# All SBUF buffers whose size is a multiple of 128 bytes begin at multiples of 128 bytes

## The chip, the cores and the metric

The kernel runs on one core of a Trainium2 chip. The metric is the device time of one execution in microseconds (us). The kernel before was timed three times: 1064.94, 1066.04 and 1066.87 us, median 1066.04 us. One more execution was recorded by the hardware profiler; all rows below come from that one.

## What is computed

A decoder trunk of two layers on 256 tokens with 1024 features, in float32. Each layer is an FFN, a token mixer and a second FFN, every one behind an RMSNorm whose scale, shift and gate come from a vector `c`:

```python
for l in range(DEPTH):                                    # 2
    mod = (c_act @ w_ada[l] + b_ada[l]).reshape(B, 3, 3, D_MODEL)
    h = ada_norm(x, norm_g[l, 0], mod[:, 0, 0], mod[:, 0, 1])
    x = x + 0.5 * mod[:, 0, 2][:, None, :] * swiglu(h, ffn_w13[l, 0], ffn_w2[l, 0])
    h = ada_norm(x, norm_g[l, 1], mod[:, 1, 0], mod[:, 1, 1])
    x = x + mod[:, 1, 2][:, None, :] * token_mixer(h, w_in[l], ...)   # NSA | FoX | MoBA heads
    h = ada_norm(x, norm_g[l, 2], mod[:, 2, 0], mod[:, 2, 1])
    x = x + 0.5 * mod[:, 2, 2][:, None, :] * swiglu(h, ffn_w13[l, 1], ffn_w2[l, 1])
return rms_norm(x, final_g)
```

`swiglu(h, w13, w2)` is `(silu(a) * b) @ w2` with `a, b = split(h @ w13)`, and the hidden width is 2816. The 256 MB that the core reads from memory are nearly all weights: every weight is used once.

## The kernel before

**Tokens and weights.** The 256 tokens are two tiles of 128, called token tile 0 and 1 (`t` in the code). Activations are the stationary operand of a matmul (loaded into TensorE by a weight load of its own), the model's weights are the moving operand (streamed through it). Each weight chunk of 128 partitions x 1024 floats (4096 bytes in each partition) is loaded into one of seven `raw` buffers by the sync engine's DMA queue. ScalarE writes its rounded high part to one of eight `whi` buffers, VectorE the remainder to one of eight `wlo` buffers (`parts`), both of type fp32r. The activations are split in the same way: `hThi0`, `hTlo0` hold the transposed normalised input of token tile 0 in eight blocks of 128 floats, `hThi1`, `hTlo1` that of token tile 1; `gThi`, `gTlo` (three buffers each) hold the transposed hidden activations of either token tile.

**A product** is three matmuls (`mm3`): high x high, high x low, low x high. In TensorE's rows a name such as `ps_pc<-wlo,hThi` gives the PSUM bank, then the moving operand (`wlo`), then the stationary one (`hThi`). Numbers at the end of a name are left out in the profile, so `hThi` stands for `hThi0` and for `hThi1`; which it is follows from the place in the program.

**Order.** FFN: eleven groups `j` of 256 hidden features. `G1(j, t, ks)` multiplies token tile `t` with `w13`: three matmuls of 512 columns for each of the blocks `k`, 24 in all for `k` = 0 to 7; `G2` multiplies the hidden activations with `w2`. In the middle of an FFN (`steady`) `G1` goes through `k` and takes the two token tiles in turn, three matmuls each, 48 in all. At an FFN's end and start (`end`, `start`), where one token tile is still being normalised, `G1` runs with one token tile alone: 24 matmuls with `hThi0`, `hTlo0` in `end` (`G1(j, 0, K8)`), then 18 with `hThi1`, `hTlo1` (`G1(j, 1, K8[2:])`). The mixer's projections (`proj`, `oproj`) also take one token tile at a time. The instructions are recorded as a list, and a planner in the kernel (`schedule`, with a table of offsets `MOVES`) sets each engine's order and which buffer of a kind is used; nothing in it looks at addresses.

**Where buffers lie.** `Program.tile` asks the pool for the buffers of a kind when the kind's name comes up for the first time. The pool puts each buffer behind the one before, at the next multiple of 32 bytes in the partition. Small buffers (a 864-byte table, many of 32, 24 or 4 bytes) stand between large ones, so large ones begin wherever the small ones leave off. In the built program the first buffer, `x0`, begins at byte 16512 = 129 x 128. Start of each kind, in bytes past a multiple of 128:

| kinds | before | after |
|---|---|---|
| `whi`, `wlo` (moving operands), `nq` | 96 | 0 |
| `hThi0`, `hTlo0` (token tile 0) | 32 | 0 |
| `hThi1`, `hTlo1` (token tile 1), `gThi`, `gTlo` | 96 | 0 |
| `onesr`, `ident`, `nk` | 64 | 0 |
| `raw`, `gate`, `ms`, `zbmo` | 32 | 0 |
| `xn`, `nf`, `sg`, `gg`, `tk`, `vals` | 96 | 0 |
| `x0`, `x1`, `ones`, `crow`, `u`, `pt` | 0 | 0 |

The blocks of `hThi` and its like begin 512 bytes apart, the two halves of a `whi` buffer 2048 bytes apart, so every block of 512 columns has its buffer's figure.

Of the kernel before, what the change touches and what calls it, by code (L numbers as in the profile page):

```python
# [7 lines left out]
F32 = mybir.dt.float32  # L8
F32R = mybir.dt.float32r
# [277 lines left out]
class Program:  # L287
# [9 lines left out]
            k.made = []  # L297

    def tile(self, pool, shape, dt, name, bufs=1, loose=False, psum=False):
        if name not in self.kinds:  # L300
            self.kinds[name] = Kind([pool.tile(shape, dt, name=f"{name}_{i}" if bufs > 1 else name)
                                     for i in range(bufs)], loose)
        kind = self.kinds[name]
        b = Buf(len(self.bufs), kind, psum)
        self.bufs.append(b)
        return View(b, kind.tiles[self.plan[1][b.i] if self.plan else 0])
# [298 lines left out]
GROUPS1 = [2, 2, 2, 1, 1]  # L605
NRAW, NHL, NMS, NPT = 7, 8, 4, 4
S0, S1 = 21, 33


@with_exitstack  # L610
# [1186 lines left out]
```

## Time and profile before

| | |
|---|---|
| three timed runs | 1064.94, 1066.04, 1066.87 us |
| the profiled execution's own time | 1065.23 us |
| its span, first to last instruction | 1063.5 us |
[...]
| read from memory | 255.96 MB, 242 GB/s over the span |
| TensorE matmuls | 5060, of them 3864 with 512 columns of fp32r |

TensorE's matmuls are pipelined: a row's duration (390 to 411 ns for 512 columns) is longer than the time from one start to the next. What a matmul costs is that step from start to start. It is read from the chain of waits, which follows the work that ended last back through the program: a piece such as "5.60 PE ps_pc x24" is 24 matmuls in a row, and 5.60 us / 24 = 233.3 ns is the step.

### The profile page before, as it was taken

What the parts mean: (1) busy time and instruction counts of PE and PEld (TensorE: products, weight loads), DVE (VectorE), ACT (ScalarE), POOL (GpSimd) and SP (SyncE); (2) the same over time, 40 slices, a digit from 0 to 9 for tenths busy, and PEclk for the clock granted to TensorE, in tenths of its full rate; (3) what the DMA queues carried; (4) which work ended last, traced back from release to release, by engine and by line L of the source; (5) the groups of instructions that cost most, each with busy time, mean ns of one, the idle gap of its engine ahead of it and who ended that gap; (6) DMA issues with size and microseconds to landing.
All of it is one profiled execution on the core that took longest, in us unless ns stands there. A gap on an engine that the chain in (4) does not pass through costs nothing.

```text
span 1063.5 us, 14643 instructions
## 1 busy us (share of the span) xinstructions
PE 1041.4 (98%) x5060; PEld 838.7 (79%) x5060; DVE 830.9 (78%) x1561; ACT 603.3 (57%) x1094; POOL 27.7 (3%) x63
## 2 busy tenths in 40 slices
PE   5999999999999999999999999999999999999997
PEld 3888888888777788788888888887877788888885
DVE  6999988779998887788587667758999778556554
ACT  5564354567887644535485444447677766444442
POOL 3000000000000100000000000000000010000000
PEclk9999999999999999999999999999999999999999
DMA  9999999567663698899548777854758247666611
GB/s 341 371 324 367 377 337 327 191 206 243 204 227 123 223 339 318 291 339 336 198 168 283 256 268 257 284 210 154 236 180 264 93 149 277 210 206 210 209 65 39
DMA packets 71468, 257.97 MB, mean 243 GB/s; under 512 B 8193, under 2 KB 8193, under 8 KB 71394
## 3 DMA queue, kind: packets, MB, share of 16 engines
q1 hardware_dynamic: 70850, 256.12, 68.8%
q0 software_dynamic: 544, 0.93, 0.4%
q8 instruction: 39, 0.64, 0.2%
q14 instruction: 35, 0.29, 0.1%
HBM read 255.96 MB, written 1.05 MB: 242 GB/s over the span
## 4 chain that ended last, share of the span: by engine, by line
PE 87%; DVE 7%; DMA 2%; ACT 2%; issue 1%; POOL 1%; SPq 0%; POOLq 0%; DVEq 0%; ACTq 0%
PE ps_pc L561 51%; PE ps_pa L561 15%; PE ps_pb L561 14%; PE ps_tr L561 7%; DVE wlo L561 3%; DMA raw<-in_w_dram 2%; DMA x<-in_x_dram 1%; ACT whi L561 1%; DVE raw L561 1%; DVE nf L561 0%; POOL ss L561 0%; DVE u L561 0%; ACT xn L561 0%; DVE hTlo L561 0%; SPq L561 0%
## 5 line engine op out<-in xcount | busy, mean ns | idle before, releaser
L561 DVE TENSOR_TENSOR wlo<-raw,whi 128x1024 fp32r<-128x1024 f32 (+1 forms) x342 | 410.8, 1216 | 129.0 <-ACT whi L561 127.4
L561 ACT ACTIVATE whi<-raw 128x1024 fp32r<-128x1024 f32 (+1 forms) x342 | 356.7, 1053 | 200.1 <-PE ps_pc L561 107.6
L561 PE MATMUL ps_pc<-whi,hThi 128*128 128x512 f32 (+1 forms) x872 | 347.6, 399 | 0.4 <-ACT gates L561 0.3
L561 PE MATMUL ps_pc<-whi,hTlo 128*128 128x512 f32 (+1 forms) x872 | 340.7, 391 | 0.0
L561 PE MATMUL ps_pc<-wlo,hThi 128*128 128x512 f32 (+1 forms) x872 | 340.5, 390 | 0.0
L561 PEld LDWEIGHTS ps_pc<-whi,hThi 128*128 128x128 f32 x872 | 163.9, 188 | 37.2 <-issue 1.8
L561 PEld LDWEIGHTS ps_pc<-whi,hTlo 128*128 128x128 f32 x872 | 163.7, 188 | 36.7 <-DVE hTlo L561 0.2
L561 PEld LDWEIGHTS ps_pc<-wlo,hThi 128*128 128x128 f32 x872 | 164.0, 188 | 33.3
L561 DVE CUSTOM_DVE_ANT_0 raw<-raw,crow 128x1024 f32<-128x1024 f32 x96 | 115.6, 1221 | 7.2 <-DMA raw<-in_wada_dram 7.2
L561 ACT ACTIVATE gThi<-ps_tr 128x256 fp32r<-128x256 f32 x88 | 32.7, 383 | 74.4 <-PE ps_tr L561 74.2
L561 ACT ACTIVATE sg<-ps_pc 128x256 f32<-128x256 f32 x82 | 31.5, 384 | 75.8 <-PE ps_pc L561 75.5
L561 PE MATMUL ps_pa<-whi,gThi 128*128 128x512 f32 x184 | 73.5, 399 | 0.0
L561 PE MATMUL ps_pb<-whi,gThi 128*128 128x512 f32 x176 | 72.4, 411 | 0.0
L561 PE MATMUL ps_pa<-whi,gTlo 128*128 128x512 f32 x184 | 72.0, 391 | 0.0
L561 PE MATMUL ps_pa<-wlo,gThi 128*128 128x512 f32 x184 | 71.8, 390 | 0.0
L561 PE MATMUL ps_pb<-whi,gTlo 128*128 128x512 f32 x176 | 69.1, 393 | 0.0
L561 PE MATMUL ps_pb<-wlo,gThi 128*128 128x512 f32 x176 | 68.7, 390 | 0.0
L561 DVE SCALAR_TENSOR_TENSOR gate<-raw,cact,gate 128x1024 f32<-128x1024 f32 x48 | 61.4, 1279 | 6.6 <-DMA raw<-in_wada_dram 6.6
L561 ACT ACTIVATE ms<-ms,nm 128x128 f32<-128x128 f32 (+1 forms) x96 | 42.6, 446 | 16.5 <-DVE nm L561 16.5
L561 DVE TENSOR_TENSOR gg<-ps_pc,sg 128x256 f32<-128x256 f32 x82 | 33.5, 420 | 20.8 <-ACT sg L561 19.6
L561 DVE TENSOR_TENSOR gTlo<-ps_tr,gThi 128x256 fp32r<-128x256 f32 x88 | 36.0, 420 | 16.9 <-ACT gThi L561 16.9
L561 PEld LDWEIGHTS ps_pa<-whi,gTlo 128*128 128x128 f32 x184 | 34.5, 188 | 7.5
(257 smaller groups left out, 1085.8 us busy)
## 6 DMA issues: line engine op xcount, KB each, us to landing
raw<-in_w_dram SPq DMA_DIRECT2D x264, 512.0 KB, 4.9
raw<-in_wada_dram SPq DMA_DIRECT2D x144, 512.0 KB, 4.8
raw<-in_win_dram SPq DMA_DIRECT2D x40, 512.0 KB, 4.3
raw<-in_wc_dram SPq DMA_DIRECT2D x16, 512.0 KB, 3.5
raw<-in_wout_dram SPq DMA_DIRECT2D x16, 512.0 KB, 5.1
raw<-in_win_dram SPq DMA_DIRECT2D x4, 426.0 KB, 3.1
x<-in_x_dram SPq DMA_DIRECT2D x2, 512.0 KB, 6.6
out_dram<-xn SPq DMA_DIRECT2D x4, 256.0 KB, 2.1
```

What stands on the lines that cost most here:

```text
L561: return getattr(self.eng, op)(*[plain(a) for a in args], **{k: plain(v) for k, v in kw.items()})
```

## The change

Before the first kind that stands in a table `HOMES` is made, all kinds of the table are made, in the table's order. The table holds all kinds whose size is a multiple of 128 bytes, and the first of them, `x0`, begins at a multiple of 128; so each begins at one. All other kinds follow behind them as before. In the built program the instructions of every engine, their order, their waits and the choice among the buffers of a kind are the same as before; only the addresses in the operands differ. The space taken is 228,352 bytes of each partition in both.

```diff
@@ -297,6 +297,10 @@
     def tile(self, pool, shape, dt, name, bufs=1, loose=False, psum=False):
+        if name not in self.kinds and name in HOMES:
+
+            for n, (s, d, b) in HOMES.items():
+                self.kinds[n] = Kind([pool.tile(s, d, name=f"{n}_{i}" if b > 1 else n) for i in range(b)], False)
         if name not in self.kinds:
             self.kinds[name] = Kind([pool.tile(shape, dt, name=f"{name}_{i}" if bufs > 1 else name)
                                      for i in range(bufs)], loose)
@@ -605,6 +609,23 @@
+HOMES = {
+    "x0": ([128, 1024], F32, 1), "x1": ([128, 1024], F32, 1), "ones": ([128, 128], F32, 1),
+    "ident": ([128, 128], F32, 1), "onesr": ([128, 128], F32R, 1), "mask": ([128, 384], F32, 1),
+    "lower": ([128, 128], F32, 1), "cmask": ([128, 2, 16], F32, 1), "vals": ([128, 2, 12, 64], F32, 1),
+    "fqk": ([128, 2, 8, 66], F32, 1), "kcT": ([128, 2, 16], F32, 1), "kcs": ([128, 2, 2, 16], F32R, 1),
+    "hexp": ([128, 2, 4, 2, 16], F32, 1), "crow": ([128, 1024], F32, 1), "gate": ([128, 1024], F32, 2),
+    "cs": ([128, 2, 2, 16], F32, 1), "xn": ([128, 1024], F32, 1), "zbmo": ([128, 4, 256], F32, 1),
+    "hThi0": ([128, 8, 128], F32R, 1), "hTlo0": ([128, 8, 128], F32R, 1), "raw": ([128, 1024], F32, 7),
+    "nf": ([128, 256], F32, 2), "whi": ([128, 1024], F32R, 8), "wlo": ([128, 1024], F32R, 8),
+    "tk": ([128, 4, 512], F32, 1), "hThi1": ([128, 8, 128], F32R, 1), "hTlo1": ([128, 8, 128], F32R, 1),
+    "sg": ([128, 256], F32, 2), "gg": ([128, 256], F32, 2), "gThi": ([128, 2, 128], F32R, 3),
+    "gTlo": ([128, 2, 128], F32R, 3), "nq0": ([128, 4, 256], F32R, 1), "nq1": ([128, 4, 256], F32R, 1),
+    "u": ([128, 512], F32, 2), "nk0": ([128, 2, 256], F32R, 1), "nk1": ([128, 2, 256], F32R, 1),
+    "vbd": ([128, 8, 64], F32, 1), "wc2": ([128, 256], F32, 1), "ra": ([128, 8, 16], F32, 1),
+    "rb": ([128, 8, 16], F32, 1), "ms": ([128, 384], F32, 4), "pt": ([128, 384], F32, 4),
+}
```

## Rows read from the trace of the kernel before

**Rows 1.** The page: busy us (share), instructions; busy tenths in 40 slices.

```profile
PE 1041.4 (98%) x5060; PEld 838.7 (79%) x5060; DVE 830.9 (78%) x1561; ACT 603.3 (57%) x1094; POOL 27.7 (3%) x63
...
PE   5999999999999999999999999999999999999997
...
PEclk9999999999999999999999999999999999999999
DMA  9999999567663698899548777854758247666611
```

**Rows 2.** TensorE's waits, whole span: us in total, times, longest.

```profile
PE ps_pc L561 <- DVE tk L561: 6.4, 1, 6.4
PE ps_pc L561 <- DMA gate<-in_c_dram: 2.3, 1, 2.3
PE ps_pc L561 <- POOL bmask L561: 2.1, 1, 2.1
PE ps_tr L561 <- ACT xn L561: 2.0, 2, 1.2
...
PE ps_pa L561 <- DVE wlo L561: 0.2, 1, 0.2
```

**Rows 3.** The page: the chain that ended last, by engine.

```profile
PE 87%; DVE 7%; DMA 2%; ACT 2%; issue 1%; POOL 1%; SPq 0%; POOLq 0%; DVEq 0%; ACTq 0%
```

**Rows 4.** Chain in order of time (start us, us, what): FFN middles, tiles in turn.

```profile
116.87 11.15 PE ps_pc L561 x48
...
445.56 11.15 PE ps_pc L561 x48
...
947.00 11.15 PE ps_pc L561 x48
```

**Rows 5.** Same view: token tile 0 alone (`hThi0`, `hTlo0`).

```profile
186.21 5.60 PE ps_pc L561 x24
...
866.27 9.80 PE ps_pc L561 x42
```

**Rows 6.** Same view: token tile 1 alone (`hThi1`, `hTlo1`).

```profile
198.88 4.08 PE ps_pc L561 x18
...
557.97 5.48 PE ps_pc L561 x24
...
882.88 6.84 PE ps_pc L561 x30
```

**Rows 7.** Same view: `G2`, stationary operand `gThi`, `gTlo`.

```profile
531.95 4.08 PE ps_pb L561 x18
```

**Rows 8.** Same view: mixer 2, `proj` of 284 columns, then `cmp_h` of 256 columns.

```profile
756.09 1.96 PE ps_pc L561 x15
758.05 3.74 PE ps_pb L561 x32
```

**Rows 9.** Stretches: us, busy (x) of PE, PEld, DVE, ACT, POOL; clock, DMA share, GB/s.

```profile
30.00:60.00 30.00, 30.00 (x131) 24.27 (x130) 29.18 (x53) 14.67 (x21) 0.00 (x0) 1.00 1.00 368
...
100.00:200.00 100.00, 100.00 (x445) 80.84 (x444) 87.73 (x136) 43.62 (x58) 0.00 (x0) 1.00 0.93 338
...
900.00:1000.00 100.00, 100.00 (x447) 80.94 (x446) 57.94 (x65) 45.27 (x60) 0.00 (x0) 1.00 0.64 214
```

**Rows 10.** VectorE by shape: busy us, mean ns of one | idle before.

```profile
L561 DVE TENSOR_TENSOR wlo<-raw,whi 128x1024 fp32r<-128x1024 f32 x336 | 405.3, 1221 | 125.5 <-ACT whi L561 123.9
...
L561 DVE TENSOR_TENSOR x<-x,u 128x512 f32<-128x512 f32 x22 | 15.1, 689 | 0.4
...
L561 DVE TENSOR_TENSOR hTlo<-xn,hThi 128x512 fp32r<-128x512 f32 x4 | 2.7, 687 | 0.7 <-ACT hThi L561 0.6
```

**Rows 11.** ScalarE by shape, same columns.

```profile
L561 ACT ACTIVATE whi<-raw 128x1024 fp32r<-128x1024 f32 x336 | 351.9, 1056 | 198.0 <-PE ps_pc L561 105.5 <-DMA raw<-in_w_dram 43.4 <-PE ps_pb L561 37.6
...
L561 ACT ACTIVATE xn<-x 128x512 f32<-128x512 f32 x24 | 15.1, 628 | 20.1 <-DVE x L561 17.7 <-DMA x<-in_x_dram 2.4
...
L561 ACT ACTIVATE hThi<-xn 128x512 fp32r<-128x512 f32 x4 | 2.5, 624 | 0.0
```

**Rows 12.** Chain of 390 to 440 us, by line.

```profile
by line: DMA raw<-in_w_dram 33.7%; DVE wlo L561 27.0%; DVE raw L561 13.8%; ACT whi L561 6.4%; issue 5.7%; DVE gg L561 3.4%; DVE gTlo L561 3.0%; PE ps_pb L561 2.8%; PE ps_pa L561 2.7%; ACT gThi L561 0.8%; PE ps_tr L561 0.5%; ACTq L561 0.2%; 
```

**Rows 13.** The page: weight loads; DMA issues (KB each, us to landing).

```profile
L561 PEld LDWEIGHTS ps_pc<-whi,hThi 128*128 128x128 f32 x872 | 163.9, 188 | 37.2 <-issue 1.8
...
raw<-in_w_dram SPq DMA_DIRECT2D x264, 512.0 KB, 4.9
```

**Rows 14.** Chain in order of time: the first DMA piece.

```profile
3.77 9.70 DMA x<-in_x_dram
```

## The prediction

> **What bounds the kernel now.** I read the page first. [...] A busy TensorE may still be a waiting one, since its durations overlap; so next its waits. They are about 14 us in total, 10.8 of them in three single waits before the first weight matmul, and a wait for `wlo` shows up once, with 0.2 us [rows 2]. The chain that ended last agrees: 87% of it is TensorE [rows 3]. So the time is, to a first approximation, the number of matmuls times the step from one start to the next, and the change can matter through that step. Everything else has cover: VectorE and ScalarE wait for each other and for TensorE (the largest wait of `whi` is for TensorE, to give a buffer free) [rows 10, 11].
>
> So I read the steps, from chain pieces that hold nothing but 512-column matmuls. With the two token tiles in turn a step is 11.15 us / 48 = 232.3 ns, at 117, at 446 and at 947 us alike [rows 4]. With token tile 0 alone it is 5.60 / 24 = 233.3 ns, and 9.80 / 42 = 233.3 ns 680 us later [rows 5]. With token tile 1 alone it is 4.08 / 18 = 226.7, 5.48 / 24 = 228.3 and 6.84 / 30 = 228.0 ns, together 16.40 / 72 = 227.8 ns [rows 6]. `G2` has 4.08 / 18 = 226.7 ns [rows 7]. These matmuls have the same shape, types and moving operand (`whi`, `wlo`), and the same order of high and low parts. A weight load takes 188 ns [rows 13], less than any step, and loads the same 128 x 128 floats in all of them. What differs is the stationary operand's address: 32 bytes past a multiple of 128 for token tile 0, 96 for token tile 1 and for `G2`, while the moving operand always lies at 96. The step does not follow the other engines: the 232.3 ns are the same in the stretch of 100 to 200 us, where DMA is busy for 0.93 and VectorE for 0.88, and in that of 900 to 1000 us with 0.64 and 0.58 [rows 4, 9]. So I take it that the place of the stationary operand against the moving one sets 5.5 ns of the step: 227.8 ns where both lie at the same distance past a multiple of 128, 233.3 ns where they don't.
>
> **The change, part by part.** No instruction is added, removed or moved, so no queue is passed and no wait added. There are only new addresses, engine by engine.
>
> TensorE: after the change moving and stationary operands all lie at 0. If the distance between them decides, all steps become 227.8 ns. The 2736 matmuls with `hThi` or `hTlo` are 1632 with the token tiles in turn (8 groups x 48 in each of three FFNs, 10 x 48 in the first one) and 1104 with one alone, 552 for each token tile.
> - Token tile 0 alone: 552 x (233.3 - 227.8) ns = 3.0 us.
> - In turn: 1632 x (232.3 - 227.8) ns = 7.3 us. The row to aim at is that of one token tile alone, since both have the operand sequence in common. At the low end only the 816 steps of token tile 0 gain, 816 x 4.5 ns = 3.7 us.
> - Token tile 1 alone and `G2` (552 + 1104 steps) stay. At the high end they, and all the others, come down to the best piece, 226.7 ns: 552 x 6.6 + 1632 x 5.6 + 552 x 1.1 ns = 13.4 us in all.
> - The 24 matmuls with `onesr` and the small shapes: 24 x 5.5 ns = 0.1 us; left out.
>
> That is 10.3 us of TensorE's time. Not all of it is on the path: of 390 to 440 us the chain runs through `raw` landing (33.7%) and `wlo` (27.0%), and hardly through TensorE [rows 12]; there a quicker matmul ends sooner and what it gains is given back as a wait for `wlo`. The same holds at the changes from one stage to the next, where the chain runs through a norm. I take the chain's share of TensorE, 87% [rows 3], as what arrives: 9.0 us.
>
> VectorE and ScalarE: their large operands move too. Rows of the same shape with operands at other places bound this: `x<-x,u`, all at 0, takes 689 ns, `hTlo<-xn,hThi`, at 96 and 32, takes 687 ns [rows 10]; `xn<-x`, read at 0, 628 ns, `hThi<-xn`, read at 96, 624 ns [rows 11]. So nothing, by -2 to +4 ns in some 340 splits of 1221 and 1056 ns, hidden behind TensorE. Without that cover 4 ns x 336 would be 1.3 us.
>
> DMA: `raw` moves from 32 to 0, `x` stays at 0. Before 17 us TensorE waits for transfers, and the chain's first DMA piece (9.70 us) is `x`, which doesn't move [rows 14]. The trace shows no large load that differs in its place alone; a chunk lands 4.9 us after its issue [rows 13]. DMA is 2% of the chain [rows 3], 21 us; a twentieth either way is 1 us. I take 0, since the engines were already at 368 GB/s from 30 to 60 us without TensorE waiting [rows 9].
>
> The sum, against the profiled execution: 1065.23 - 9.0 = 1056.2 us. The median of the three runs lies 0.8 us above that execution, so the forecast is **1057 us**, with its own range from 3.0 + 3.7 us x 0.87 = 5.8 us of gain (1060) to 13.4 us (1052.6).
>
> [...] What the rows show is two steps for two places, 227.8 and 233.3 ns [rows 5, 6]. [...]
>
> **The rivals.**
>
> *Not the place past 128, but something that comes with the token tile* (15%). `hThi0` and `hTlo0` lie right below `raw`, `hThi1` and `hTlo1` some 110 KB higher, behind `wlo`; the two could differ by region, and the change moves no large buffer by more than 4 KB. For it: the two steps are known from two or three sets of buffers only. Against it: `G2` serves both token tiles at 226.7 ns. Then the time is 1066, within 0.2%.
>
> *The place of the stationary operand by itself* (10%, slower). A start at 96 could be the good one whatever the moving operand does, and a start at 0 be like 32. Then token tile 1 and `G2` lose what token tile 0 would have gained: (552 + 1104) x 5.5 ns = 9.1 us, and 1632 x (233.3 - 232.3) ns = 1.6 us in turn, 10.7 us on the engine and 9.3 us at 87%: 1075 us. It decides as soon as more than half of the steps with weights now at 96 get longer by over 4 ns. Against it: the chain piece of `cmp_h`, whose stationary operands begin at all multiples of 16 bytes in turn, has 3.74 / 32 = 116.9 ns for 256 columns [rows 8], no longer in proportion than the others.
>
> *The moving operand's place costs, too* (10%, much faster). [...]
>
> *A part of that* (9%): the step goes below the best piece, by up to 4 ns in all 3864 matmuls, 13 us more than the forecast: 1045 to 1052 us.
>
> **How the numbers follow.** The forecast has 56%, its neighbour below 9%, much faster 10%, no change 15%, slower 10%. Predicted is 1057 us. The range holds the forecast, the neighbour and no change, 80%: 1045 to 1067.5 us; the forecast's own is 1052 to 1061. About 0.2% (2 us) is what a measurement of this kernel can tell from no change. Faster by more: 56 + 9 + 10 = 75%; the same 15%; slower 10%.
>
> **What would show it.** Right: the pieces of token tile 0 alone at 186 and 866 us come down from 233.3 to about 228 ns, those in turn (48 matmuls) from 11.15 to about 10.95 us, those of token tile 1 and of `G2` stay; VectorE's and ScalarE's means stay within 5 ns; new short waits for `wlo` near 400 us take a part. Wrong: if token tile 0 keeps 233.3 ns, the place past 128 was not it; if all go to 233, a start at 0 is a bad one; if all fall below 226, the moving operand's place had its price as well.

## The result: 1057.4 us, and the profile after

The changed kernel took 1057.41 us (median of 4 runs, 1056.77 to 1057.61); the kernel before, measured beside it, 1066.39 us (4 runs, 1064.94 to 1066.87). The ratio is 0.9917, with a 95% interval of 0.9900 to 0.9934: 9.0 us faster. The profiled executions are 7.6 us apart: 1065.23 us before, 1057.61 after, and in spans 1063.5 and 1055.9. The mean granted clock of TensorE over the span is 0.998 in both.

The page of the changed kernel: the span, busy us (share) and instructions of each engine, and the chain that ended last, by engine.

```profile
span 1055.9 us, 14643 instructions
...
PE 1032.2 (98%) x5060; PEld 837.9 (79%) x5060; DVE 830.0 (79%) x1561; ACT 602.8 (57%) x1094; POOL 27.7 (3%) x63
...
PE 81%; DVE 12%; DMA 2%; issue 2%; ACT 2%; POOL 1%; POOLq 0%; DVEq 0%; ACTq 0%
```

Busy shares say nothing here: 98% against 98% before [rows 1]. The busy time of TensorE is 9.2 us less with the same 5060 matmuls. VectorE, ScalarE and the weight loads moved by less than 1 us. The chain is the second thing to read: TensorE's share of it fell from 87% [rows 3] to 81%, and VectorE's rose from 7% to 12%. A faster TensorE meets the splitting of the weights more often.

Where TensorE became faster is read in the chain of waits in order of time (start us, us, what), in the pieces that answer to [rows 4 to 7]: token tile 0 alone, token tile 1 alone, in turn, `G2`, and 860 us into the program token tile 0 and 1 again.

```profile
184.26 5.47 PE ps_pc L565 x24
...
196.86 4.08 PE ps_pc L565 x18
...
443.99 10.90 PE ps_pc L565 x48
...
529.34 4.08 PE ps_pb L565 x18
...
861.16 9.52 PE ps_pc L565 x42
...
877.47 6.84 PE ps_pc L565 x30
```

Token tile 0 alone went from 5.60 us to 5.47 for 24 matmuls, so from 233.3 ns to 227.9 ns a step, and from 9.80 to 9.52 for 42 (226.7 ns). In turn it went from 11.15 to 10.90 us for 48 (227.1 ns). Token tile 1 alone keeps 4.08 for 18 and 6.84 for 30, `G2` keeps 4.08: the same figures as [rows 6, 7]. So what had been long is now as short as the rest, and the rest is not touched.

Over all steps, not only those on the chain: the starts of the 512-column weight matmuls in the trace, one to the next, as means over all steps up to 245 ns (the longer ones, some 200, stand beside a shorter matmul such as a transpose, or hold a wait):

| | before | after |
|---|---|---|
| token tile 0 alone | 233.3 ns | 228.7 ns |
| tiles in turn | 232.1 ns | 227.6 ns |
| token tile 1 alone | 228.5 ns | 228.2 ns |
| `G2` alone | 228.3 ns | 228.3 ns |
| all 512-column steps up to 245 ns | 230.8 ns | 227.9 ns |
| steps over 245 ns: their excess over 230 ns, summed | 22.4 us | 24.7 us |

With the counts of the program, 552 x 4.6 ns + 1632 x 4.5 ns = 9.9 us of TensorE's time were saved. Some 2.3 us of them came back, nearly all of it as longer waits ahead of a shorter matmul, and 7.5 us remained at the last matmul (which starts at 1055.5 us before and at 1048.0 after). Half of what came back lies in the stretch of 390 to 440 us. Its row of before, and then that of after (us, busy (x) of PE, PEld, DVE, ACT, POOL; clock, DMA share, GB/s):

```profile
390.00:440.00 50.00, 49.86 (x220) 39.82 (x218) 40.27 (x57) 24.66 (x32) 0.00 (x0) 1.00 0.88 310
```

```profile
390.00:440.00 50.00, 48.75 (x220) 39.47 (x219) 39.44 (x55) 25.07 (x32) 0.00 (x0) 1.00 0.88 312
```

TensorE was idle for 0.14 us of it before and for 1.25 us after, with 220 matmuls in both. The timeline of TensorE has the place: the last matmul of a product, and the transposes of `gg` (the hidden activations, which VectorE makes) that come behind it. Before, then after:

```profile
422.83 0.39 PE L561 MATMUL ps_pa<-whi,gTlo 128*128 128x512 f32 x1
423.26 0.44 PE L561 MATMUL ps_tr<-ident,gg 128*128 128x128 f32 x2
```

```profile
420.46 0.39 PE L565 MATMUL ps_pa<-whi,gTlo 128*128 128x512 f32 x1
422.02 0.44 PE L565 MATMUL ps_tr<-ident,gg 128*128 128x128 f32 x2 [1.17 <-DVE gg L565]
```

TensorE came to this place 2.4 us earlier than before and left it 1.2 us earlier. The chain of waits says why `gg` was not there. Before, then after, the landing of a weight chunk and VectorE's `gg` behind it:

```profile
413.32 5.99 DMA raw<-in_w_dram
...
422.88 0.67 DVE gg L561 x2
```

```profile
411.57 6.49 DMA raw<-in_w_dram
...
421.62 0.67 DVE gg L565 x2
```

The chunk lands at 419.31 us before and at 418.06 after. Behind it VectorE makes the chunk's `wlo`, works through one more chunk, and then makes `gg`. All this came only 1.25 us earlier, so the rest of TensorE's lead was waited away.

VectorE and ScalarE of the changed kernel, the shapes of [rows 10, 11] (busy us, mean ns of one, idle before):

```profile
L565 DVE TENSOR_TENSOR wlo<-raw,whi 128x1024 fp32r<-128x1024 f32 x336 | 404.8, 1220 | 120.9 <-ACT whi L565 119.8
...
L565 DVE TENSOR_TENSOR x<-x,u 128x512 f32<-128x512 f32 x22 | 15.0, 687 | 0.4
```

```profile
L565 ACT ACTIVATE whi<-raw 128x1024 fp32r<-128x1024 f32 x336 | 351.9, 1057 | 195.2 <-PE ps_pc L565 100.5 <-DMA raw<-in_w_dram 41.4 <-PE ps_pb L565 38.7
```

1220 ns against 1221 and 1057 against 1056: their operands moved too, and it cost and gave nothing. (`x` and `u` lie at 0 past a multiple of 128 in both: 687 ns against 689.) One more thing did change. Of 16 to 27 us, when every DMA engine is busy (share 1.02 and 1.03), the rows of before and of after are:

```profile
16.00:27.00 11.00, 10.34 (x38) 8.16 (x39) 10.24 (x15) 5.90 (x9) 0.00 (x0) 1.00 1.03 410
```

```profile
16.00:27.00 11.00, 10.46 (x40) 8.27 (x41) 10.24 (x15) 5.92 (x9) 0.00 (x0) 1.00 1.02 419
```

The last number is GB/s: 419 against 410. So there are two candidates for the gain, the step and the transfers, and one open question about the step: which relation of the two addresses counts.

### The profile page after: what moved, and what is told of

Same layout as the page of the kernel before. It is cut to its first block, busy times and chain, and to the rows that moved or that the text cites. A ratio compares the mean times of both kernels' runs of the same rounds, so it can differ in the third digit from the quotient of the medians.

```text
span 1055.9 us, 14643 instructions
## 1 busy us (share of the span) xinstructions
PE 1032.2 (98%) x5060; PEld 837.9 (79%) x5060; DVE 830.0 (79%) x1561; ACT 602.8 (57%) x1094; POOL 27.7 (3%) x63
## 4 chain that ended last, share of the span: by engine, by line
PE 81%; DVE 12%; DMA 2%; issue 2%; ACT 2%; POOL 1%; POOLq 0%; DVEq 0%; ACTq 0%
PE ps_pc L565 47%; PE ps_pa L565 14%; PE ps_pb L565 13%; PE ps_tr L565 6%; DVE wlo L565 4%; DVE raw L565 2%; DMA raw<-in_w_dram 1%; DVE gate L565 1%; ACT whi L565 1%; DVE nf L565 1%; DMA raw<-in_win_dram 1%; DMA raw<-in_wada_dram 1%; POOL ss L565 0%; DVE u L565 0%; DVE ms L565 0%
## 5 line engine op out<-in xcount | busy, mean ns | idle before, releaser
L565 PE MATMUL ps_pc<-wlo,hThi 128*128 128x512 f32 (+1 forms) x872 | 337.1, 387 | 0.0
```

Source lines behind the costliest of these rows:

```text
L565: return getattr(self.eng, op)(*[plain(a) for a in args], **{k: plain(v) for k, v in kw.items()})
```

## The experiments

The theory on record was that the distance between the stationary and the moving operand counts, past a multiple of 128 bytes. Its rivals now: the distance counts past a larger power of two; the place of the stationary operand by itself; the region of the partition in which it lies; the transfers. Past a multiple of 256 bytes, `whi` and `wlo` lie at 96 before, `hThi1`, `hTlo1`, `gThi` and `gTlo` at 96 too, and `hThi0` and `hTlo0` at 160; after, all lie at 0. `raw` goes from 160 to 0. Each kernel below was timed against the kernel before on the same chip (1065.8 to 1066.2 us).

### The kernel before, with token tile 0's buffers moved

A pad ahead of `hThi0` moves `hThi0` and `hTlo0` only; a second one ahead of `raw` fills up to 512 bytes, so that everything behind keeps its place past a multiple of 512. Nothing else of the kernel before is changed.

```diff
     def tile(self, pool, shape, dt, name, bufs=1, loose=False, psum=False):
+        if name not in self.kinds and name in PADS:
+            pool.tile([128, PADS[name] // 4], F32, name=f"pad_{name}")
...
+PADS = {'hThi0': 64, 'raw': 448}      # t0_64
+PADS = {'hThi0': 192, 'raw': 320}     # t0_192
```

By the 64 bytes token tile 0 comes to 96 past a multiple of 128, as `whi` has it, but 128 bytes from it past a multiple of 256. By the 192 bytes it comes to the place of `whi` past any power of two up to 512.

> The layout of before, with 64 unused bytes ahead of hThi0 and 448 ahead of raw, so that hThi0 and hTlo0 (the stationary operands of token tile 0) lie 96 bytes past a multiple of 128, as the moving operands whi and wlo do; all other buffers keep their distance past a multiple of 512. Past a multiple of 512 the stationary operands of token tile 0 are at 224 and the moving ones at 352. Theory A (the distance between stationary and moving operand counts, past multiples of 128): token tile 0 alone falls from 233.3 to about 228 ns per matmul, 1057 to 1058 us. Theory B (the distance counts, but past 256 or 512): token tile 0 keeps 233 ns, 1066 us. Theory C (only a start at a multiple of 128 is good): no large operand of a weight matmul begins at one, 1066 us.

Measured: 1064.92 us (10 runs, 1064.22 to 1067.67), ratio 0.9995, interval 0.9986 to 1.0005. The chain of waits, tile 0 alone and in turn:

```profile
186.89 5.58 PE ps_pc L563 x24
...
446.79 11.13 PE ps_pc L563 x48
```

5.58 / 24 = 232.5 ns and 11.13 / 48 = 231.9 ns: 0.8 and 0.4 ns less than before, nowhere near 228. Equal places past 128 don't do it. The theory as it was written, with its 128, fell here.

> As the run before, but with 192 bytes ahead of hThi0 and 320 ahead of raw: the stationary operands of token tile 0 now lie 352 bytes past a multiple of 512, exactly as the moving ones. Theories A and B: token tile 0 alone at about 228 ns, 1057 to 1058 us, the whole gain of the change with nothing aligned to 128. Theory C: 233 ns and 1066 us.

Measured: 1056.65 us (4 runs, 1055.59 to 1057.80), ratio 0.9909, interval 0.9895 to 0.9924. The same view:

```profile
185.18 5.44 PE ps_pc L563 x24
...
495.26 10.88 PE ps_pc L563 x48
```

226.7 ns and 226.7 ns. With two buffers moved, both 96 bytes past a multiple of 128 as in `t0_64`, and nothing aligned that was not aligned before, the whole gain of the change is there. So alignment is not what it was about, and the other 75 buffers of the table have no part in it that these runs can tell.

### The changed kernel, with everything moved by 32 bytes

```diff
             for n, (s, d, b) in HOMES.items():
+                if n in PADS:
+                    pool.tile([128, PADS[n] // 4], F32, name=f"pad_{n}")
                 self.kinds[n] = Kind([pool.tile(s, d, ...) ...], False)
...
+PADS = {'x0': 32}
```

All kinds of the table begin 32 bytes past a multiple of 128, at the same distances from each other as in the changed kernel.

> The changed kernel with 32 unused bytes ahead of its first buffer: every buffer of the table begins 32 bytes past a multiple of 128, with all distances between them as in the changed kernel. Theories A and B: all steps 227 to 229 ns as in the changed kernel, 1057 to 1058 us. Theory C: the steps go back to 231 to 233 ns or above, 1066 to 1076 us. If raw's place matters to the transfers, the first dense matmuls begin some 0.4 us later than in the changed kernel (where 4096-byte packets went at 419 GB/s from 12 to 30 us, against 410 before).

Measured: 1059.66 us (4 runs, 1058.59 to 1060.09), ratio 0.9936, interval 0.9921 to 0.9951. The chain:

```profile
185.42 5.47 PE ps_pc L567 x24
...
480.42 10.90 PE ps_pc L567 x48
```

The steps are those of the changed kernel, with no buffer aligned to 128. So the place of the stationary operand by itself has no price: 0, 32 and 96 (token tile 1 before) all give about 228 ns as long as the moving operand has the same place. The time is 2.3 us above the changed kernel's, though, and above the 1057 to 1058 us expected. In the profiled executions the excess of the steps over 245 ns sums up to 27.0 us here against 24.7 us, about that difference; but it is 24.3 us in `raw_0` below against 22.4 us before, and there the time does not differ. The transfers run at 409 GB/s of 16 to 27 us; the runs with `raw` below speak against them as the cause. What makes these 2 us stays open.

### The changed kernel, with only the stationary operands moved

The stationary kinds go to the end of the table, behind a pad. All else of the changed kernel stays at multiples of 128.

```diff
+LAST_KINDS = ("onesr", "hThi0", "hTlo0", "hThi1", "hTlo1", "gThi", "gTlo")
+HOMES = {n: v for n, v in HOMES.items() if n not in LAST_KINDS} | {n: HOMES[n] for n in LAST_KINDS}
...
+PADS = {'onesr': 64}      # stat_64; 0, 128, 256, 32, 192 in the others
```

> The changed kernel with all stationary operands of the weight matmuls (onesr, hThi0, hTlo0, hThi1, hTlo1, gThi, gTlo) moved behind all other buffers of the table and 64 bytes ahead of them: moving operands at 0, stationary ones at 64 past a multiple of 512. Theories A and B: every 512-column step goes to about 233 ns, 3840 steps longer by 5 ns, 19 us on the engine and 16 to 19 us in time: 1073 to 1077 us. Theory C in the form that the moving operand's start counts: no change against the changed kernel, 1057 us.

Measured: 1075.05 us (4 runs, 1073.19 to 1076.09), ratio 1.0079, interval 1.0062 to 1.0096. The chain, token tile 0 alone, token tile 1 alone, in turn and `G2`:

```profile
188.55 5.60 PE ps_pc L567 x24
...
201.37 4.20 PE ps_pc L567 x18
...
449.82 11.20 PE ps_pc L567 x48
...
537.07 4.20 PE ps_pb L567 x18
```

All four are at 233.3 ns, token tile 1 and `G2` as well, which had never been long before. The step goes with the distance, for any stationary buffer. But the buffers also lie in another region now; the control is the same order with no pad.

> Control: the changed kernel with the stationary operands (onesr, hThi0, hTlo0, hThi1, hTlo1, gThi, gTlo) moved to the end of the table, behind all other large buffers, with nothing ahead of them. Moving and stationary operands are all at 0 past a multiple of 512, as in the changed kernel, but token tile 0's stationary operands lie 140 KB higher. Theory B (the distance past a multiple of 256 or 512): steps of 227 to 229 ns, 1055 to 1058 us. Rival (the region of the memory): another step for token tile 0, a time that differs from the changed kernel's by some us.

Measured: 1058.02 us (4 runs, 1057.88 to 1058.76), ratio 0.9924, interval 0.9909 to 0.9938, and in the chain:

```profile
184.64 5.46 PE ps_pc L567 x24
...
443.99 10.90 PE ps_pc L567 x48
```

These are the changed kernel's steps at other ends of the partition, so the region is out.

> As the control, with 128 unused bytes ahead of the stationary operands: every buffer of the table still begins at a multiple of 128, moving operands at 0 and stationary ones at 128 past a multiple of 512. Theory B: every step about 233 ns and 1073 to 1077 us, slower than the kernel before though all buffers are aligned to 128. Theory A (128 is what counts): 1055 to 1058 us as the control.

Measured: 1070.79 us (4 runs, 1069.56 to 1071.26), ratio 1.0040, interval 1.0025 to 1.0055. The chain, token tile 0, token tile 1, in turn:

```profile
186.97 5.58 PE ps_pc L567 x24
...
199.73 4.19 PE ps_pc L567 x18
...
447.20 11.16 PE ps_pc L567 x48
```

This is the run that parts the change's words from its effect. Every buffer that the change speaks of begins at a multiple of 128 bytes here, exactly as its description asks, and the kernel is slower than the one before. The steps are 232.5 to 232.8 ns; their mean over the program is 232.4, about 1 ns below those of 64 bytes, so the time lies somewhat under that of `stat_64`, and under the 1073 to 1077 us expected. `t0_64` has the same distance of 128 with the moving operands at 96, and the same step for token tile 0 alone, 232.5 ns.

> As the control, with 256 unused bytes ahead of the stationary operands: moving operands at 0, stationary ones at 256 past a multiple of 512. If the distance counts past multiples of 256: 227 to 229 ns and 1055 to 1058 us. If it counts past multiples of 512: about 233 ns and 1073 to 1077 us.

Measured: 1056.40 us (4 runs, 1056.23 to 1058.09), ratio 0.9906, interval 0.9890 to 0.9923:

```profile
872.26 5.47 PE ps_pc L567 x24
...
924.50 10.90 PE ps_pc L567 x48
```

At 256 bytes the step is as short as at 0, at 128 it is not. So the distance counts past a multiple of 256 bytes, not of 128 and not of 512.

> As the control with the stationary operands behind all others, with 32 unused bytes ahead of them: distance 32. If only a distance of 0 past a multiple of 256 is good: 232 to 233.5 ns and 1070 to 1076 us. If conflicts grow with the distance: less, 229 to 231 ns and 1060 to 1066 us.

Measured: 1074.26 us (2 runs, 1073.02 to 1075.50), ratio 1.0076, interval 1.0056 to 1.0095, and in the chain:

```profile
188.02 5.60 PE ps_pc L567 x24
...
450.21 11.19 PE ps_pc L567 x48
```

233.3 and 233.1 ns: 32 bytes cost as much as 64.

> As the run before, with 192 unused bytes: distance 192, which is also 64 short of the next multiple of 256. If only a distance of 0 past a multiple of 256 is good: 232 to 233.5 ns and 1070 to 1076 us. If what matters is whether the stationary operand lies ahead of the moving one or behind it, another step than the 233.4 ns of distance 64.

Measured: 1061.61 us (3 runs, 1060.35 to 1061.79), ratio 0.9954, interval 0.9939 to 0.9968, and in the chain:

```profile
185.67 5.49 PE ps_pc L567 x24
...
198.27 4.12 PE ps_pc L567 x18
...
444.75 10.99 PE ps_pc L567 x48
```

228.8, 228.9 and 229.0 ns. So it is not a distance of 0 alone that is good: 192 bytes are nearly as good as none, though 192 is no nearer to a multiple of 256 than 64 is. All distances together, stationary minus moving, as means over all 512-column steps up to 245 ns:

| distance past a multiple of 256 | 0 (`stat_0`) | 0 (`stat_256`) | 32 | 64 | 128 | 192 |
|---|---|---|---|---|---|---|
| step, ns | 227.9 | 227.9 | 233.2 | 233.4 | 232.4 | 229.2 |
| time, us | 1058.0 | 1056.4 | 1074.3 | 1075.1 | 1070.8 | 1061.6 |

The price is not the same on both sides of 0: the stationary operand 32 or 64 bytes past the moving one is the worst, 192 (which is -64) is nearly harmless. That side has one distance only, and a few matmuls give a hint that its neighbour is not harmless: `onesr`, stationary in 24 matmuls, lies at 224 (which is -32) from its moving operand before and in `t0_192`, and their steps have means of 232.7 and 232.4 ns there, against 228.8 in `stat_0` and 228.0 in `stat_256`.

### The changed kernel, with only the low parts of the activations moved

```diff
+LAST_KINDS = ("hTlo0", "hTlo1", "gTlo")
+PADS = {'hTlo0': 64}
```

One of three matmuls of a product has a stationary operand at a distance of 64, the other two at 0. If each matmul pays for its own operand alone, the mean step is a third of the way from 227.9 to 233.4 ns.

> The changed kernel with only the low parts of the stationary operands (hTlo0, hTlo1, gTlo, a third of all weight loads) moved 64 bytes away from the moving operands' place; high parts and moving operands at 0. If a step is lengthened by the weight load that runs beside it (the load for the next matmul), the matmuls wlo x hThi and wlo x gThi, beside which the low parts are loaded, get 5 ns longer and those with whi x hTlo do not. If it is lengthened by the stationary operand that the matmul itself uses, it is whi x hTlo that gets longer. Either way about 1280 steps x 5.5 ns = 7 us on the engine and 1063 to 1065 us.

Measured: 1067.11 us (8 runs, 1065.46 to 1068.06), ratio 1.0010, interval 0.9999 to 1.0020. The mean step is 231.1 ns, more than the 229.8 ns of a third, and the time is above the 1063 to 1065 us expected, so a displaced operand also costs the matmuls beside it. Which they are is read against their order. In this run's timelines of TensorE and of its weight loads (start us, us, what), the displaced `hTlo` is loaded while `wlo` x `hThi` runs:

```profile
500.27 0.39 PE L567 MATMUL ps_pc<-wlo,hThi 128*128 128x512 f32 x1
500.50 0.40 PE L567 MATMUL ps_pc<-whi,hTlo 128*128 128x512 f32 x1
500.74 0.39 PE L567 MATMUL ps_pc<-whi,hThi 128*128 128x512 f32 x1
```

```profile
500.27 0.19 PEld L567 LDWEIGHTS ps_pc<-whi,hTlo 128*128 128x128 f32 x1
```

TensorE's rows by shape (busy us, mean ns of one), first the changed kernel, then this one:

```profile
L565 PE MATMUL ps_pc<-whi,hThi 128*128 128x512 f32 x840 | 335.6, 400 | 0.1
L565 PE MATMUL ps_pc<-whi,hTlo 128*128 128x512 f32 x840 | 328.0, 391 | 0.0
L565 PE MATMUL ps_pc<-wlo,hThi 128*128 128x512 f32 x840 | 327.8, 390 | 0.0
```

```profile
L567 PE MATMUL ps_pc<-whi,hThi 128*128 128x512 f32 x840 | 335.6, 400 | 0.1
L567 PE MATMUL ps_pc<-whi,hTlo 128*128 128x512 f32 x840 | 332.9, 396 | 0.0
L567 PE MATMUL ps_pc<-wlo,hThi 128*128 128x512 f32 x840 | 329.8, 393 | 0.0
```

The matmul that uses the displaced operand lasts 5 ns longer, the one ahead of it, beside which the operand is loaded, 3 ns; the one behind it lasts as long as before. The steps say the same but for the last: from the start of `whi` x `hTlo` to the next start it is 234.7 ns on average against 227.8 in the changed kernel, 229.7 against 227.6 for the one ahead and 229.1 against 227.9 for the one behind. So most falls on the matmul that uses the operand, and a third on its neighbours. It shows in [rows 4 to 6] as well: in turn, three steps of 228 and three of 233 ns would make 230.6 ns on average, but the step of before was 232.3 ns. With the trace's matmuls put beside the program's order, token tile 0 has a mean of 232.8 ns there and token tile 1, whose own operands lie at a distance of 0, has 231.6 ns.

### `raw` alone: is any of the gain the transfers'?

In the layout of before, pads move `raw` to a multiple of 512 and leave all operands of matmuls where they were; then the same together with `t0_192`.

```diff
+PADS = {'raw': 352, 'mods': 160}                  # raw_0
+PADS = {'hThi0': 192, 'raw': 160, 'mods': 160}    # t0_raw
```

> The layout of before, with 352 unused bytes ahead of raw and 160 behind it, so that only the seven raw buffers (the transfers' targets) move, from 160 to 0 past a multiple of 512; everything else keeps its distance past a multiple of 512. The steps should stay at 233.3 ns for token tile 0 alone and 230.8 ns on average. Transfers: from 16 to 27 us, where they are dense, 419 to 421 GB/s as in every kernel here with raw at 0, against 409 to 410 with raw at 32 or 160. If transfers that are 2.4% quicker shorten the kernel, as far as the chain's DMA share of 2% goes, 0.5 us; else 0. So 1065.4 to 1066 us and no clear difference in time.

Measured: 1066.50 us (11 runs, 1064.44 to 1067.92), ratio 1.0003, interval 0.9995 to 1.0012. Its row of 16 to 27 us (same columns as above):

```profile
16.00:27.00 11.00, 10.45 (x36) 8.14 (x37) 10.24 (x15) 5.99 (x9) 0.00 (x0) 1.00 1.02 419
```

419 GB/s against 410: the faster transfers of the changed kernel come from the place of `raw`, and by the interval they are worth 0.5 us at most.

> The two moves together in the layout of before: hThi0 and hTlo0 to the moving operands' place (352 past a multiple of 512) and raw to 0. If the distance (steps) and raw's place (transfers) are all that the change brings, this has the whole of it: steps of 228 ns, 419 to 421 GB/s from 16 to 27 us, 1055.5 to 1057.5 us, the changed kernel's time within its interval.

Measured: 1057.82 us (4 runs, 1057.15 to 1058.86), ratio 0.9920, interval 0.9904 to 0.9935. Its steps have a mean of 227.9 ns and it moves 420 GB/s of 16 to 27 us; still it is no faster than `t0_192` (1056.65, with `raw` at its old place), and 0.3 us above the range expected. So the whole gain is the step's, as far as these runs can tell. No version here is faster than the changed kernel beyond its interval: 0.9909 (`t0_192`), 0.9906 (`stat_256`) and 0.9917 overlap.

## Why the prediction came out

**What bounds the kernel: right.** The prediction went by the step from start to start and not by the busy share. The busy share of TensorE stayed at 98% while the time fell by 0.8%.

**The distance between the operands sets the step: right in kind, wrong in its measure.** The step that failed is the sentence that both must lie "at the same distance past a multiple of 128". `t0_64` has that and is not faster; `stat_128` has every buffer on a multiple of 128 and is slower than before. What counts is the distance past a multiple of 256 bytes. The rows that the prediction read could not part the two, since they held two distances only, 0 and 64, and these are the same by either measure. That the change reaches 0 past 256 as well is luck: from `xn` to `nq1` every size in the table is a multiple of 512, so all these buffers have the same place past 512 as `xn` has. Of the stationary operands of these matmuls only `onesr` lies at 128, and the steps of its 24 matmuls still have a mean of 234 ns. A table in another order could have met the description and made the kernel slower, as `stat_128` shows; the prediction had no rival for that.

**Token tile 0 alone, 3.0 us.** 4.6 ns in place of 5.5 over all its steps, so 552 x 4.6 = 2.5 us. The chain's pieces show the full 5.4 ns (233.3 to 227.9); the other steps are a little longer.

**In turn, 7.3 us.** 1632 x 4.5 = 7.3 us: as forecast. Its aim, the row of one token tile alone, was the right one. (Four of the ten groups of the first FFN, 192 of these matmuls, take the token tiles in blocks of up to 12 and not three by three; by the prediction's own prices that is 0.3 us less.)

**Token tile 1 and `G2` stay: right** (4.08 us for 18 in both).

**What arrives, 87%: too high in the traces, open in the times.** In the profiled pair 7.5 of 9.9 us, 76%, arrived. The experiments have less than 87% as well: from `stat_0` to `stat_128`, 3864 steps x 4.5 ns are 17.4 us on the engine and 12.8 us in the time (73%), and to `stat_64` it is 17.0 of 20.9 us (81%). The medians of the timed runs are 9.0 us apart, as forecast, but their interval, 7.0 to 10.7 us, holds either share. The chain's share of TensorE was taken as the part that arrives, but it is read at the old speed; when TensorE is quicker, that share itself falls (to 81%). The place named for it was right, 390 to 440 us, the wait was not: the prediction had TensorE wait for `wlo`, and that wait is 0.2 us in all before and after. What grew there is the wait for `gg`, 1.2 us, which VectorE makes only behind a chunk's `wlo`. The forecast of the profiled execution was 1056.2 us and it took 1057.6. The median came out near the predicted 1057 because that execution lies 0.2 us above its median, where the prediction had counted 0.8 us the other way. So two misses, of 1.4 and of 1.0 us, nearly cancel there, and that is luck.

**VectorE, ScalarE, no price: right**, within 2 ns. **DMA, no price: right.** That the transfers became 2% quicker (419 GB/s against 410) was not foreseen; `raw_0` shows that this gives nothing that can be told from 0.

**The rivals.** "Something that comes with the token tile" fell with `t0_192` and `stat_0`. "The place of the stationary operand by itself" fell with the result and with `all_32`. "The moving operand's place costs, too" fell with the result: with the moving operand at 0, 32 and 96 past 128 and the stationary one at the same place, 24 matmuls on the chain take 227.9 ns a step (the changed kernel), 227.9 (`all_32`) and 226.7 (`t0_192`). "A part of that" fell with it: no piece of 18 or more 512-column matmuls in the chains read here is below 226.7 ns a step. No run shows a place of the moving operand that makes the step shorter than that; the 10% and the 9% given to it were the author's estimate.

**What stays open.** Why the distance counts was not found. The step goes with the distance between the operand of the weight load and the operand that is streamed (227.9 ns at 0, 233.4 at 64), and with neither's place alone (both at 0, at 32 or at 96 past a multiple of 128: about 228 ns). `lo_64` speaks against the simplest explanation, that a load lengthens the matmul it runs beside: the load of the displaced operand takes 0.19 us, all beside the matmul ahead, and that one's step grew by 2 ns, while the step of the matmul that uses the operand, when the load is over, grew by 7. What links the two operands is not shown by any run.

## What to carry to other kernels

Where two groups of matmuls of the same shape have different steps, compare the addresses of their operands before anything else, and compare the stationary with the moving one, not either with a round number. Here two pads of 192 and 320 bytes gave all that the new layout of 77 buffers gave. And when a layout is changed, test the relation that is thought to count by breaking it alone: the same alignment with another distance made this kernel slower than it had been.

## What the runs showed of the hardware

- For fp32r matmuls of 512 columns, each with a weight load of 128 x 128 ahead of it, the step depends on the distance of the stationary from the moving operand, past a multiple of 256 bytes: 227.9 ns at 0 (`stat_0`, and `stat_256`), 233.2 at 32, 233.4 at 64, 232.4 at 128, 229.2 at 192 (`stat_32` to `stat_192`). The range is 2.4% of the step, and over 3864 matmuls 17 us of this kernel's time (1058.0 to 1075.1).
- A displaced stationary operand lengthens not only the matmul that uses it (step of 234.7 ns against 227.8) but its neighbours too: the one ahead (229.7 against 227.6), beside which it is loaded, and the one behind (229.1 against 227.9), in `lo_64` against the changed kernel.
- DMA rows of 4096 bytes that are written to multiples of 512 in the partition moved at 417 to 421 GB/s of 16 to 27 us, where the DMA share is 1.02 to 1.03 (nine kernels: the changed one, the six with `stat`, `raw_0` and `t0_raw`), those written at 160 past it at 410 and 409 (before and `t0_192`), at 32 past it at 409 (`all_32`). That is 2%; what makes it is not shown.
- The splits of 1024 elements on VectorE and ScalarE took as long with their operands at 32 and 96 past a multiple of 128 as at 0: 1221 and 1220 ns, 1056 and 1057 ns (before and after).
